# Picking the experts' inputs with the one-hot matrix stationary, and other edits at the ends of the stages

## The chip, the cores and the metric

The program runs on one core of a Trainium2 chip. The metric is the device time of one execution in microseconds (us). Each kernel is timed in several runs; one more execution is taken by the hardware profiler, and the rows below come from it. TensorE multiplies, with its weight loads beside it (PEld); VectorE (DVE), ScalarE (ACT) and GpSimd (POOL) work on the tiles; SyncE (SP) and GpSimd issue most of the transfers (DMA).

## The reference

One layer of an encoder on 256 tokens of 2048 channels, all in float32:

```
h = rms_norm(x) ; proj = h @ w_in
q, k, v, q_idx, k_idx, w_idx | r, d_w, kr, vr, d_a, d_g = split_cols(proj)
y_dsa  = sparse attention: 8 heads of 128; an indexer keeps the best min(256, L/4) = 64
         keys of each query, chunks of 64, RMS-norm and rotary on q and k
y_rwkv = RWKV-7: 16 heads of 64; token shift, decay and gates of low rank;
         state = state * w + (state @ -kk) b^T + v k^T ; y = state @ r
x = x + concat(y_dsa, y_rwkv) @ w_out
t = rms_norm(x)
grp = top-1 of 4 groups ; two of its 4 experts, weights p_grp * p_exp / sum
x = x + sum over 16 experts e of combine[:, e] * ((silu(t @ gate_e) * (t @ up_e)) @ down_e)
```

An expert is three matrices of 2048 x 512, 512 x 2048 for the last; the sixteen together are 201 MB and are read in every run.

## The kernel before

**Order of the work.** TensorE's instructions are in an order that the program writes out by hand, while it is built; the other engines' orders are planned around it. A small planner (`Order`, L45) keeps a clock that each product moves on by an assumed price. `drive` (L399) goes through the stream of weight tiles (a task is one such tile with its 6 or 12 products) and between two tasks lets every chain go on whose time or event has come: the RWKV block chains (`rwkv_early`, `rwkv_late`), the attention, the norms. A chain's `yield` is either a wait in us (the list `Y`) or the name of an event. A task can need events (`od.need`); then the planner steps its clock and writes out what the chains have, with no task between.

**RWKV.** Eight blocks of two heads. `rwkv_early(b)` makes the products `pa` (L605) and hands a triangular system to `solve` (L653): it goes out to DRAM by GpSimd's queue, comes back spread over the lanes, is solved in 62 operations of GpSimd, goes out again and comes back as `XT` (L669). `solve` sets the event `solved{b}` SOLVE_US = 54 us later on the planner's clock (L670). `rwkv_late(b)` waits for it; its first product, `pz` on `XT` (L688), is the first use. Only one late chain is under way at a time. `rwkv_early(b)` waits for `late{b-2}` in its middle (L558). A late chain ends in a tile `r{b}` of the output projection's input, split into two parts (L899 and L900).

**Output projection.** The 2048 input channels stand in sixteen slots, `YSLOTS`: r0 to r5, h0 to h3, r6, h4 to h7, r7 (r for RWKV's blocks, h for the attention's heads). The 2048 output columns are done in four groups `c0` to `c3` of sixteen tasks, six products of 512 columns each; a task needs its slot's event. AHEAD = 10: the stream takes ten tasks of c0, ten of c1, and then the last six of each (L197).

**Experts.** After the projection come the norm, the routing and, while VectorE routes, WARM products that compute nothing. Each expert gets 64 slots of tokens; experts go in eight pairs, and a one-hot matrix `sel` (tokens x 128 slots) picks a pair's tokens. `gather(p)` (L1323) makes the turned inputs in four quarters of 512 channels: 8 products of a tile of the residual stream `uu` (128 x 128, stationary) with `sel` (128 columns, moving), both in float32, then a scale by `gF` on VectorE into `xe` (L1338); and at the end the turned `sel` and the factors. `up(p)` (L1356) has four quarters `kg`, each with 8 products for `gate` and 8 for `up`, and calls the generators of `gather` in between: the first two quarters of a pair are picked ahead of the down projection of the pair before, the others inside `up`. `down` (L1390) turns the hidden tile and makes four groups `pd` of 512 columns; `scatter` (L1409) brings them back to the tokens with products on two exact parts (`yh`, `yl`, type float32r) and adds them to `x1`. Output leaves by SyncE's queue.

**Weights.** The experts' weights come as 192 tiles of 1 MB, 24 a pair, in a ring (`load_chunk`, L1079): EB = 20 lasting places and three that are used once. A tile's transfer waits for the product that read its place last. The first tiles are loaded in the background of the projections, GpSimd's queue issuing; once the experts run, SyncE's. The last four tiles go in quarters.

What the program writes between `up(p)` and the next pair:

```
up(p, pend)
if p < 7:
    next(turns[p + 1])
    next(turns[p + 1])
_, selT, sv = got.pop(p)
```

Of the kernel before, what the change touches and what calls it, by code (L numbers as in the profile page):

```python
# [31 lines left out]
AHEAD = 10  # L32
EB1, EB2, EB = 9, 4, 20
# [3 lines left out]
PACE, SOLVE_US, RSTD_US = 2.2, 54.0, 16.1  # L37
# [80 lines left out]
def block_kernel(ctx: ExitStack, tc: tile.TileContext, a: dict, dbg=None):  # L118
# [960 lines left out]
    def load_chunk(i, gate=False):  # L1079
# [3 lines left out]
        elif i in once:  # L1083
            t = wp.tile([P, 2048], F32, name="ewr", tag="rawA")
        elif k < 3:
            t = gp.tile([P, 2048], F32, name="ew0", tag=f"g{k}")
        elif k < EB1:
            t = ewp[1].tile([P, 2048], F32, name="ew", bufs=EB1 - 3)
        elif k < EB1 + EB2:
            t = ewp[2].tile([P, 2048], F32, name="ew2", bufs=EB2)  # L1090
        elif k < EB1 + EB2 + 4:
            t = big.tile([P, 2048], F32, name="ewh", tag=f"h{k - EB1 - EB2}")
        elif k < EB1 + EB2 + 6:
            t = wp.tile([P, 2048], F32, name="eww", tag=f"w2{k - EB1 - EB2 - 4}")
        else:
            t = ewp[3].tile([P, 2048], F32, name="ew3", bufs=EB - EB1 - EB2 - 6)
# [43 lines left out]
    def u_chain(cc, ps):  # L1140
        cs = slice(cc * 512, (cc + 1) * 512)
        uu, lg, us = mo_["uu"], mo_["lg"], mo_["us"]
        for j in range(2):
            o = uu[:, j, cs]
            DVE.tensor_tensor(out=o, in0=o, in1=ps[j], op=ALU.add)
            sq = us.tile([P, 512], F32, name="usq", bufs=1)
            ACT.activation(out=sq, in_=o, func=AF.Square, accum_out=mo_["ssq"][:, j, cc:cc + 1])
        yield Y[34] if cc == 0 else Y[35]
        uT = us.tile([P, 4, T], F32, name="uT", bufs=1)
        for j in range(2):  # L1150
# [3 lines left out]
            ACT.copy(out=uT[:, :, j * P:(j + 1) * P], in_=pt.rearrange("p (i t) -> p i t", i=4))  # L1154
            if j == 0 and cc < 3:
                yield Y[20]
        yield Y[21]
# [73 lines left out]
    mx, sums, mxe, sme = sm_("mx", 1), sm_("sums", 4), sm_("mxe", 4), sm_("sme", 4)  # L1231
    ge = l[:, :, 4:20].rearrange(g4, g=4)
# [3 lines left out]
    DVE.tensor_tensor(out=l[:, :, 0:4], in0=l[:, :, 0:4], in1=mx.broadcast_to([P, 2, 4]), op=ALU.subtract)  # L1236
    DVE.tensor_tensor(out=ge, in0=ge, in1=mxe.rearrange(bc, o=1).broadcast_to([P, 2, 4, 4]), op=ALU.subtract)
# [60 lines left out]
    ewp[3] = ctx.enter_context(tc.tile_pool(name="ew3", bufs=1, reuse_waits="tile"))  # L1298
# [10 lines left out]
    def experts():  # L1309
# [13 lines left out]
        def gather(p):  # L1323

            sel = md.tile([P, 2, P], F32, name="sel")
            for e in range(2):
                for j in range(2):
                    DVE.tensor_scalar(sel[:, j, e * 64:(e + 1) * 64], iota, pos[:, j, 2 * p + e:2 * p + e + 1], selm[:, j, 2 * p + e:2 * p + e + 1], ALU.is_equal, ALU.mult)  # L1328
            xe = []
            got[p] = [xe, None, None]  # L1330
            for kq in range(4):
# [5 lines left out]
                t = XE[0][:, (kq % 2) * 512:(kq % 2 + 1) * 512].rearrange("p (a t) -> p a t", t=P)  # L1337
                DVE.tensor_tensor(out=t, in0=ps.rearrange("p (a t) -> p a t", t=P),  # L1338
                                  in1=gF[:, 4 * kq:4 * kq + 4].rearrange("p (a o) -> p a o", o=1).broadcast_to([P, 4, P]), op=ALU.mult)
                xe.append(t)  # L1340
                yield
            ps = misc()
            for j in range(2):
                tr(ps[:, j * P:(j + 1) * P], sel[:, j, :])
            for j in range(2):
                mm(ps[:, T:T + 17], sel[:, j, :], val[:, j, :], start=(j == 0), stop=(j == 1))
            selT = md.tile([P, T], F32R, name="selT")
            sv = md.tile([P, 2], F32, name="sv", bufs=2)
            ACT.copy(out=selT, in_=ps[:, 0:T])  # L1349
            DVE.tensor_copy(sv[:, 0:1], ps[:, T:T + 1])  # L1350
            for e in range(2):
                DVE.tensor_copy(sv[64 * e:64 * e + 64, 1:2], ps[64 * e:64 * e + 64, T + 1 + 2 * p + e:T + 2 + 2 * p + e])
            got[p][1:] = selT, sv
            yield

        def up(p, pend):  # L1356
            pgt = pg_.tile([P, 512], F32, name="gate", bufs=1)
            put = pg_.tile([P, 512], F32, name="up", bufs=1)
            for kg in range(4):
                w = {}  # L1360
                xe = got[p][0]
                for m, o in ((0, pgt), (1, put)):
# [13 lines left out]
                if kg < 2:  # L1376
                    next(turns[p])
                if kg == 1:
                    next(turns[p])
            sv = got[p][2]  # L1380
            if not R:
                R.append(wp.tile([P, 2048], F32, name="R", tag="rawA"))
                XE[0] = R[0][:, 1024:2048]
                Y2.append(wp.tile([P, 1024], F32R, name="Y2", tag="rawB"))
# [5 lines left out]
        def down(sv):  # L1390
            hh, hT = R[0][:, 0:512], R[0][:, 512:1024]
            yh, yl = Y2[0][:, 0:512], Y2[0][:, 512:1024]
# [4 lines left out]
            for n in range(4):  # L1397
                pd = pg_.tile([P, 512], F32, name="pd", bufs=2)
                w = [nxt() for _ in range(2)]
                for kt in range(4):  # L1400
                    if kt == 2:
                        yield n
# [6 lines left out]
        def scatter(selT, n, first, final):  # L1409
            yh, yl = Y2[0][:, 0:512], Y2[0][:, 512:1024]  # L1410
            ns = slice(n * 512, (n + 1) * 512)
            for j in range(2):
                ps = pg_.tile([P, 512], F32, name="sc", bufs=2)
# [3 lines left out]
                if final:  # L1417
                    SP.dma_start(out=outv[:, j, ns], in_=x1[j][:, ns])
# [4 lines left out]
        next(turns[0])  # L1423
        pend = None
        for p in range(8):
            up(p, pend)
            if p < 7:
                next(turns[p + 1])
                next(turns[p + 1])
            _, selT, sv = got.pop(p)  # L1430
            prev = None
            for n in down(sv):
                if prev is not None:
# [5 lines left out]
        scatter(*pend, False, True)  # L1439
# [112 lines left out]
```

## Time and profile before

| | us |
|---|---|
| median of 3 runs | 1066.7 (1066.42 to 1069.66) |
| the profiled execution | 1065.43 |
| its span, first to last instruction | 1063.3 |
| TensorE busy | 1015.9 (96%) |
| VectorE busy | 536.6 (50%) |
| ScalarE busy | 386.4 (36%) |
| GpSimd busy | 287.2 (27%) |
| moved by DMA | 298.75 MB, mean 281 GB/s |

The span lies inside the execution's time. The projections and the mixers take it up to about 590 us, the experts run from 605 us to the end. A busy time says that an engine worked, not that something waited for it; for that the timelines, the waits and the chain of work are read. In a timeline row the bracket at the end is the idle time of the engine ahead of the instruction, with what ended it.

### The profile page before, as it was taken

The numbers are of one execution on the slowest core, as the hardware profiler recorded it, in microseconds if no ns is written. First come the engines' busy times: TensorE is split into PE (matmuls) and PEld (weight loads), VectorE is DVE, ScalarE is ACT, GpSimd is POOL, SyncE is SP. The second block draws the span as 40 slices with busy tenths as digits, with TensorE's granted clock in tenths as the row PEclk, the third lists the DMA queues.
The fourth block names the chain that finished last, engine by engine and source line by source line (L and its number), as shares of the span: only waits on it lengthen the run. The fifth ranks groups of instructions, "written<-read, shape, count | busy, mean of one in ns | idle before, by whom it ended". The sixth has DMA issues, their size and how long they took to land.

```text
span 1063.3 us, 17241 instructions
## 1 busy us (share of the span) xinstructions
PE 1015.9 (96%) x6466; PEld 685.3 (64%) x6466; DVE 536.6 (50%) x1195; ACT 386.4 (36%) x816; POOL 287.2 (27%) x705
## 2 busy tenths in 40 slices
PE   7899999999999999799899899999999999999997
PEld 6888988887888987687678644444444444444432
DVE  5796868697958786956444413122221223131313
ACT  6755655666557674656344201010000000010101
POOL 4106672658166825573043110000000000000000
PEclk9999999999999999999999999999999999999999
DMA  9556654454546554456389999999999999999995
GB/s 310 194 184 182 185 162 159 113 161 117 166 140 182 156 148 136 128 164 210 98 302 349 421 420 371 419 421 419 419 421 419 421 419 420 420 419 420 420 415 206
DMA packets 61754, 298.75 MB, mean 281 GB/s; under 512 B 8960, under 2 KB 12336, under 8 KB 37600
## 3 DMA queue, kind: packets, MB, share of 16 engines
q1 hardware_dynamic: 51264, 251.21, 63.7%
q0 software_dynamic: 10400, 46.36, 12.3%
q8 instruction: 53, 0.87, 0.3%
q14 instruction: 37, 0.30, 0.1%
HBM read 294.37 MB, written 3.15 MB: 280 GB/s over the span
## 4 chain that ended last, share of the span: by engine, by line
PE 73%; DVE 4%; ACT 2%; issue 1%; DMA 1%; ACTq 0%; DVEq 0%
PE pp L131 23%; PE pd L131 11%; PE gate L131 11%; PE up L131 10%; PE misc L131 6%; PE sc L131 3%; PE pz L131 2%; PE py L131 2%; DVE W L207 1%; DMA RB<-wo 1%; ACT W L206 1%; PE pc L131 1%; PE lps L131 1%; PE yps L131 1%; PE misc L141 1%
## 5 line engine op out<-in xcount | busy, mean ns | idle before, releaser
L131 PE MATMUL pp<-W,hT 128*128 128x512 f32 x768 | 189.7, 398 | 1.6 <-DVE W L207 1.6
L131 PE MATMUL pp<-hT,W 128*128 128x256 f32 x1296 | 171.6, 289 | 12.3 <-ACT W L206 8.6
L207 DVE TENSOR_TENSOR W<-RA,W 128x512 fp32r<-128x512 f32 x200 | 137.8, 695 | 83.6 <-ACT W L206 82.1
L131 PEld LDWEIGHTS pp<-hT,W 128*128 128x128 f32 x1296 | 161.7, 194 | 17.1 <-ACT W L206 8.8
L206 ACT CAST W<-RA 128x512 fp32r<-128x512 f32 x200 | 123.1, 620 | 119.9 <-PE pp L131 87.4
L131 PEld LDWEIGHTS pp<-W,hT 128*128 128x128 f32 x768 | 141.2, 189 | 32.1 <-DVE W L207 2.0
L131 PE MATMUL pp<-W,yT 128*128 128x512 f32 x384 | 95.5, 403 | 3.5 <-ACT yT L899 3.3
L666 POOL TENSOR_TENSOR xt<-xt,tt 128x24 f32<-128x24 f32 (+23 forms) x248 | 91.8, 370 | 19.3
L664 POOL TENSOR_TENSOR tt<-xt,at 128x24 f32<-128x24 f32 (+23 forms) x248 | 86.0, 347 | 40.0 <-DMA at<-din 21.3
L207 DVE TENSOR_TENSOR W<-RB,W 128x512 fp32r<-128x512 f32 x100 | 69.3, 696 | 43.7 <-ACT W L206 42.1
L131 PEld LDWEIGHTS pp<-W,yT 128*128 128x128 f32 x384 | 72.1, 192 | 20.7 <-ACT yT L899 3.5
L206 ACT CAST W<-RB 128x512 fp32r<-128x512 f32 x100 | 61.5, 619 | 64.6 <-PE pp L131 51.3
L131 PE MATMUL pd<-ew,R 128*64 128x512 f32 x352 | 81.1, 598 | 2.7 <-ACT R L1396 2.7
L131 PE MATMUL up<-ew,R 128*64 128x512 f32 x352 | 79.3, 592 | 0.0
L131 PEld LDWEIGHTS misc<-sel,uu 128*128 128x128 f32 x512 | 59.6, 192 | 15.2 <-issue 13.8
L1406 ACT ACTIVATE Y<-pd,sv 128x512 fp32r<-128x512 f32 x32 | 22.0, 687 | 126.9 <-PE pd L131 126.9
L1407 DVE SCALAR_TENSOR_TENSOR Y<-pd,sv,Y 128x512 fp32r<-128x512 f32 x32 | 24.0, 750 | 83.1 <-ACT Y L1406 83.1
L131 PE MATMUL misc<-sel,uu 128*128 128x128 f32 x512 | 63.0, 278 | 0.7 <-DVE sel L1328 0.7
L1416 DVE TENSOR_TENSOR x<-x,sc 128x512 f32<-128x512 f32 x56 | 36.0, 684 | 55.0 <-PE sc L131 55.0
L131 PE MATMUL gate<-ew,R 128*64 128x512 f32 x272 | 61.7, 595 | 0.0
L1338 DVE TENSOR_TENSOR R<-misc,gF 128x512 f32<-128x512 f32 x28 | 19.4, 692 | 79.5 <-PE misc L131 79.5
L1349 ACT CAST selT<-misc 128x256 fp32r<-128x256 f32 x8 | 3.0, 372 | 154.5 <-PE misc L131 154.5
(383 smaller groups left out, 1253.6 us busy)
## 6 DMA issues: line engine op xcount, KB each, us to landing
ew<-we SPq DMA_DIRECT2D x66, 1024.0 KB, 19.9
ew<-wdn SPq DMA_DIRECT2D x38, 1024.0 KB, 18.7
ew<-we POOLq DMA_DIRECT2D x25, 1024.0 KB, 10.6
ewh<-we SPq DMA_DIRECT2D x24, 1024.0 KB, 17.8
RA<-wd SPq DMA_DIRECT2D x43, 512.0 KB, 3.6
RA<-wr SPq DMA_DIRECT2D x35, 512.0 KB, 4.5
RB<-wd SPq DMA_DIRECT2D x21, 512.0 KB, 3.7
RA<-wo SPq DMA_DIRECT2D x21, 512.0 KB, 4.1
```

The source lines that it names most:

```text
L131: PE.matmul(out, lhsT=lhsT, rhs=rhs, start=start, stop=stop, skip_group_check=skip)
L141: PE.transpose(out=out, in_=in_, identity=ident)
L206: ACT.copy(out=hi, in_=raw)
L207: DVE.tensor_tensor(out=lo, in0=raw, in1=hi.bitcast(F32), op=ALU.subtract)
L664: POOL.tensor_tensor(out=tv, in0=xt[:, 0:n, s_:s_ + 1].broadcast_to([P, n, m]), in1=at[s_ >= 8][:, s_ % 8 if s_ < 8 else s_ - 8, s_ + 1:32 ...
L666: POOL.tensor_tensor(out=xt[:, 0:n, s_ + 1:32], in0=xt[:, 0:n, s_ + 1:32], in1=tv, op=ALU.subtract)
L1338: DVE.tensor_tensor(out=t, in0=ps.rearrange("p (a t) -> p a t", t=P), in1=gF[:, 4 * kq:4 * kq + 4].rearrange("p (a o) -> p a o", o=1).broa ...
L1349: ACT.copy(out=selT, in_=ps[:, 0:T])
L1406: ACT.activation(out=yh, in_=pd, func=AF.Copy, scale=sv[:, 1:2])
L1407: DVE.scalar_tensor_tensor(out=yl, in0=pd, scalar=sv[:, 1:2], in1=yh.bitcast(F32), op0=ALU.mult, op1=ALU.subtract)
L1416: DVE.tensor_tensor(out=x1[j][:, ns], in0=(uu[:, j, ns] if first else x1[j][:, ns]), in1=ps, op=ALU.add)
```

## The change

- `gather`: pairs 0 and 1 keep the old pick (`direct`; pair 1 for its first half). From then on a quarter of `uu` is first split into two exact parts of type float32r (`parts`: a copy on ScalarE, a difference on VectorE, for each half of the tokens); `pick` has `sel` stationary and moves the parts, four products of 512 columns, ScalarE copies the result, `turned` transposes it in four products, and VectorE scales as before. The generator's steps are called at other places of `up`.
- Pair 0's first quarter is scaled in two halves.
- The pool of split parts takes the place of one ring slot: EB from 20 to 19.
- SOLVE_US from 54 to 47, AHEAD from 10 to 14.
- In the last group of the output projection the sums of squares come after the turned tiles, and the second copy is on VectorE. The routing has two VectorE operations fewer.
- The last down group goes in two halves of 256 columns; the output's second half of the tokens leaves by ScalarE's queue.

```diff
-AHEAD = 10
-EB1, EB2, EB = 9, 4, 20
+AHEAD = 14
+EB1, EB2, EB = 9, 4, 19
-PACE, SOLVE_US, RSTD_US = 2.2, 54.0, 16.1
+PACE, SOLVE_US, RSTD_US = 2.2, 47.0, 16.1
...
+        if cc == 3:
+            for j in range(2):
+                squares(j)
...
-    DVE.tensor_reduce(mx[:, :, 0], l[:, :, 0:4], axis=AX.X, op=ALU.max)
-    DVE.tensor_reduce(mxe, ge, axis=AX.X, op=ALU.max)
...
+    DVE.tensor_reduce(mx5, l5, axis=AX.X, op=ALU.max)
...
+            def parts(kq):
+
+                two = []
+                for j in range(2):
+                    t, o = md.tile([P, 2, 512], F32R, name="two", bufs=2), uu[:, j, kq * 512:(kq + 1) * 512]
+                    ACT.copy(out=t[:, 0, :], in_=o)
+                    DVE.tensor_tensor(out=t[:, 1, :], in0=o, in1=t[:, 0, :].bitcast(F32), op=ALU.subtract)
+                    two.append(t)
+                return two
+
+            def pick(two):
+
+                ps = misc()
+                for j in range(2):
+                    for n in range(2):
+                        mm(ps, sel_r[:, j, :], two[j][:, n, :], start=(j == 0 and n == 0), stop=(j == 1 and n == 1))
+                E = wp.tile([P, 512], F32, name="E", tag="rawB")
+                ACT.copy(out=E, in_=ps)
+                return E
+
+            def turned(kq, E):
+                ps = misc()
+                for i in range(4):
+                    tr(ps[:, i * P:(i + 1) * P], E[:, i * P:(i + 1) * P])
+                xe.append(scaled(kq, ps, 0, 4))
...
+            else:
+                two = parts(0)
+                yield
+                E = pick(two)
+                two = parts(1)
+                yield
+                turned(0, E)
+                E = pick(two)
+                two = parts(2)
+                turned(1, E)
             yield
...
+                E = pick(two)
+                two = parts(3)
+                yield
+                turned(2, E)
+                yield
+                E = pick(two)
+                factors()
+                yield
+                turned(3, E)
+                yield
...
-                        if p == 0 and kg == 0:
-                            next(turns[0])
+                        if p == 0 and kg == 0 or p and kg == 1:
+                            next(turns[p])
+                        if kg == 2 and p:
+                            next(turns[p])
+                        if kg == 2 and p < 7:
+                            next(turns[p + 1])
+                        if kg == 3 and p < 7:
+                            next(turns[p + 1])
...
+                if final and n == 3:
+                    for hf in range(2):
+                        cs = slice(hf * 256, hf * 256 + 256)
...
-                    SP.dma_start(out=outv[:, j, ns], in_=x1[j][:, ns])
+                    (SP, ACT)[j].dma_start(out=outv[:, j, ns], in_=x1[j][:, ns])
```

## Rows read from the trace of the kernel before

**Rows 1.** The page's slices: what the transfers moved in each of 40 slices.
```profile
GB/s 310 194 184 182 185 162 159 113 161 117 166 140 182 156 148 136 128 164 210 98 302 349 421 420 371 419 421 419 419 421 419 421 419 420 420 419 420 420 415 206
```

**Rows 2.** Windows: stretch, length, busy time of the engines, granted clock, DMA share, GB/s.
```profile
440.00:460.00 20.00, 14.46 (x89) 11.54 (x87) 15.76 (x34) 7.13 (x17) 8.45 (x14) 0.83 0.42 116
520.00:540.00 20.00, 14.42 (x111) 10.78 (x110) 6.77 (x15) 5.65 (x15) 6.30 (x17) 0.83 0.41 136
...
650.00:655.00 5.00, 5.00 (x24) 1.87 (x22) 2.04 (x3) 0.69 (x1) 0.00 (x0) 1.00 0.71 259
...
960.00:1020.00 60.00, 59.33 (x312) 27.26 (x308) 14.04 (x26) 4.40 (x7) 0.00 (x0) 1.00 1.01 420
...
1047.00:1048.00 1.00, 1.00 (x6) 0.34 (x6) 1.00 (x2) 0.00 (x0) 0.00 (x0) 1.00 0.40 143
```

**Rows 3.** Timeline of TensorE, 446 to 545: start, duration, instruction [idle before it].
```profile
446.10 0.89 PE L131 MATMUL pa<-G 64*64 64x128 f32 x24 [0.96 <-DVE G L584]
...
503.98 5.74 PE L131 MATMUL pp<-W,yT 128*128 128x512 f32 x24
509.56 1.05 PE L131 MATMUL pz<-R,XT 128*128 128x128 f32 x8
510.45 2.78 PE L131 MATMUL yps<-PT,vt 128*128 128x256 f32 x16
512.99 1.64 PE L131 MATMUL pp<-W,yT 128*128 128x512 f32 x6
...
522.91 0.33 PE L131 MATMUL pS<-S,Ph 64*64 64x64 f32 x4 [0.40 <-ACT S L727]
...
532.07 11.96 PE L131 MATMUL pp<-W,yT 128*128 128x512 f32 x42 [3.27 <-ACT yT L899]
```

**Rows 4.** Timeline: block 0's solve on TensorE and GpSimd, block 7's on GpSimd.
```profile
74.54 1.10 PE L131 MATMUL pa<-G 64*64 64x128 f32 x32
...
122.98 2.21 POOL L669 DMA_DIRECT2D XT<-dout  x4 [3.80 <-DMA dout<-xt]
...
129.89 1.05 PE L131 MATMUL pz<-R,XT 128*128 128x128 f32 x8
...
490.17 2.18 POOL L669 DMA_DIRECT2D XT<-dout  x4 [3.84 <-DMA dout<-xt]
```

**Rows 5.** The tile `XT`, 50 to 160: from issue to landing.
```profile
DMA to landing us min/median/max: 2.5/3.3/3.9
```

**Rows 6.** Timeline of TensorE around the down projections of two successive pairs.
```profile
866.18 3.84 PE L131 MATMUL misc<-sel,uu 128*128 128x128 f32 x32
869.86 0.60 PE L141 MATMUL misc<-ident,R 128*128 128x128 f32 x4
871.13 5.37 PE L131 MATMUL pd<-ew,R 128*64 128x512 f32 x24 [0.68 <-ACT R L1396]
876.43 1.20 PE L131 MATMUL sc<-Y,selT 128*128 128x512 f32 x4
...
922.09 3.84 PE L131 MATMUL misc<-sel,uu 128*128 128x128 f32 x32
```

**Rows 7.** Timeline: SyncE's issues of weights, TensorE's first down groups of the last pair.
```profile
651.19 5.51 SPq L1106 DMA_DIRECT2D ewh<-we  x4
...
1009.05 7.79 SPq L1106 DMA_DIRECT2D ew<-wdn  x4
...
1036.19 5.37 PE L131 MATMUL pd<-ew,R 128*64 128x512 f32 x24 [0.68 <-ACT R L1396]
```

**Rows 8.** DMA issues, 1003 to 1018: tile, count, KB, median us to landing.
```profile
ew<-wdn SPq DMA_DIRECT2D x4, 1024.0 KB, 19.9
```

**Rows 9.** The chain of work that ended last: the first scale of the experts.
```profile
607.23 0.70 DVE XE L1338
```

**Rows 10.** Timeline of VectorE at the end.
```profile
1056.11 1.28 DVE L1416 TENSOR_TENSOR x<-x,sc 128x512 f32<-128x512 f32 x2 [0.59 <-PE sc L131]
```

**Rows 11.** The tensor `out`: from issue to landing.
```profile
DMA to landing us min/median/max: 2.3/3.3/6.0
```

More of the change, by code (lines that the diff above doesn't have):

```diff
@@ L1142, in u_chain, with squares @@
         uu, lg, us = mo_["uu"], mo_["lg"], mo_["us"]
+        def squares(j):
+            sq = us.tile([P, 512], F32, name="usq", bufs=1) if cc < 3 else ppbank()
+            ACT.activation(out=sq, in_=uu[:, j, cs], func=AF.Square, accum_out=mo_["ssq"][:, j, cc:cc + 1])
         for j in range(2):
@@ L1342, in gather @@
[L1342 to L1352, printed above, removed]
@@ new lines, in factors @@
+            def factors():
+                ps = misc()
+                for j in range(2):
+                    tr(ps[:, j * P:(j + 1) * P], sel[:, j, :])
+                for j in range(2):
+                    mm(ps[:, T:T + 17], sel[:, j, :], val[:, j, :], start=(j == 0), stop=(j == 1))
+                selT = md.tile([P, T], F32R, name="selT")
+                sv = md.tile([P, 2], F32, name="sv", bufs=2)
+                ACT.copy(out=selT, in_=ps[:, 0:T])
+                DVE.tensor_copy(sv[:, 0:1], ps[:, T:T + 1])
+                for e in range(2):
+                    DVE.tensor_copy(sv[64 * e:64 * e + 64, 1:2], ps[64 * e:64 * e + 64, T + 1 + 2 * p + e:T + 2 + 2 * p + e])
+                got[p][1:] = selT, sv
@@ L1379, in up @@
                     next(turns[p])
+                    if p == 0:
+                        next(turns[p])
             sv = got[p][2]
@@ L1399, in down @@
                 w = [nxt() for _ in range(2)]
+                if final and n == 3:
+                    for hf in range(2):
+                        cs = slice(hf * 256, hf * 256 + 256)
+                        for kt in range(4):
+                            if kt == 2 and hf == 0:
+                                yield n, 0, 512
+                            for e in range(2):
+                                mm(pd[64 * e:64 * e + 64, cs], hT[:, kt * P + 64 * e:kt * P + 64 * e + 64], w[e][:, kt * 512 + hf * 256:kt * 512 + hf * 256 + 256], start=(kt == 0), stop=(kt == 3))
+                        ACT.activation(out=yh[:, cs], in_=pd[:, cs], func=AF.Copy, scale=sv[:, 1:2])
+                        DVE.scalar_tensor_tensor(out=yl[:, cs], in0=pd[:, cs], scalar=sv[:, 1:2], in1=yh[:, cs].bitcast(F32), op0=ALU.mult, op1=ALU.subtract)
+                    yield n, 0, 256
+                    break
                 for kt in range(4):
                     if kt == 2:
-                        yield n
+                        yield n, 0, 512
                     for e in range(2):
@@ L1422, in experts @@
         turns = [gather(p) for p in range(8)]
-        next(turns[0])
+        for _ in range(3):
+            next(turns[0])
         pend = None
@@ L1428, in experts @@
                 next(turns[p + 1])
-                next(turns[p + 1])
             _, selT, sv = got.pop(p)
             prev = None
-            for n in down(sv):
-                if prev is not None:
+            for n, c0, c1 in down(sv, p == 7):
+                if c1 < 512:
+                    scatter(selT, n, False, True, c0, c1)
+                elif prev is not None:
                     if not base and p == 0 and n == 1:
@@ L1438, in experts @@
             pend = prev
-        scatter(*pend, False, True)
+        scatter(*pend, False, True, 256, 512)
     experts()
```

70 lines of the change are left out of this document (45 added, 25 removed).

## The prediction

> **What bounds the kernel now.** I read the page's slices first: from the 23rd slice on, the transfers move 420 GB/s and never more [rows 1], and the windows of the expert stage show the same 420 GB/s with TensorE busy 59.33 of 60 us at full clock [rows 2]. So two things run side by side there, and it matters which is ahead. One pair of experts takes 24 tiles of weights of 1 MB; SyncE issues one each 2.49 us (four in 7.79, of which the last takes 0.33) [rows 7], so a pair's weights need 59.8 us, while TensorE needs 55.9 us: the pick ahead of the down projection recurs at 866.18 and 922.09 [rows 6]. TensorE therefore eats up its stock of loaded tiles by 3.9 us a pair. At the end little is left: the two tiles of the last pair's second down group are issued last at 1016.5 and land 19.9 us later [rows 7, 8], at 1036.4; TensorE starts on them about 1039.7 (16 of the 24 instructions that begin at 1036.19) [rows 7]. The stock is 3.3 us deep there, and the last bytes land at 1047 [rows 2]. **Whatever TensorE saves in the expert stage, 3.3 us of it can show, unless the stream itself ends sooner.**
>
> Ahead of the experts TensorE works almost without a break, but for two holes: 440 to 460 and 520 to 540, in each of which it is busy only 14.4 of 20 us and the granted clock is 0.83 [rows 2], that is (1 - 0.83) x 20 / 0.5 = 6.8 us at 1.2 GHz. The second hole is the last block's late chain: tiles of the output projection that need no late result run out, TensorE idles, and goes on at 532.07 when the last head's result is split (ACT yT) [rows 3]. Idle: 20 - 14.42 = 5.6 us. After it 42 instructions take 11.96 us, where 24 took 5.74 [rows 3], so 42 should take 10.0: 1.9 us lost to the lower level. Together 7.5 us.
>
> The profiled run took 1065.4 us (span 1063.3); the median of the timed runs is 1066.7, so 1.3 us go onto the result of the sum.
>
> **The change, part by part.**
>
> *Planner constants* (SOLVE_US 54 to 47). The planner puts a block's late chain 54 us after its triangular solve is sent off; for block 0 this is real time: products `pa` end at 75.6, the first product on the solve's result starts at 129.9, 54.3 later [rows 4]. With 47 it is written 7 us earlier, at 122.6 plus up to a tile, say 123.5. But the solve's result is sent at 122.98 in four transfers of 0.55 us issue, which land up to 3.9 us after issue [rows 4, 5], so about 128.4. TensorE is in order: it stands 4.9 us (4.0 to 5.5), and the projection's tiles queued behind this product stand with it. A hole of 5.6 us cost 1.9 more by the clock; I add the same: +6.8. Block 7 has its `pa` done at 447.0, its result sent at 490.2 to 492.4, so landed by 496, 49 us after, and used at 509.56, 63 us after [rows 3 to 5]; 7 us less costs such a block nothing. What it gives: block b+2 starts only when late b is done, so every second block gains another 7 us: late 1, 3, 5, 7 by 7, 14, 21, 28 on the planner's clock, less the 6.8 lost at block 0, so the last one some 20 us. Then the hole at 520 to 540 has filler: -7.5.
>
> *AHEAD 10 to 14.* The output projection now asks for heads h4 to h6 of the attention as its 12th to 14th tile and not after 20. Those heads' products stand at 510.45, and their tile follows directly at 512.99 [rows 3]: they come just in time for the 22nd tile now. Asked for ten tiles (ten times 1.43 = 14 us) sooner, less the 7 to 14 us of late products that now stand before, they are late by up to 7 us or not at all; the planner then writes the rest of the chain without filler. Bounds 0 and 12.2 (the late chain without filler, 522.5 to 532.07, is 9.6 long [rows 3]; with the clock's 1.9, and 0.7 for one more round of the heads, 12.2); I take 4.5, nearer to zero, because those heads run through TensorE and need no round over GpSimd.
>
> *The hole at 440 to 460* comes from ScalarE and VectorE, crowded by late 5, early 7 and the attention at once. Late 5 now ends some 14 us sooner (21 less 6.8). Bounds: all of it stays (0), or all goes (5.5 + 1.9 = -7.4); I take -4.8. **Front: -7.5 + 6.8 + 4.5 - 4.8 = -1.0** (between -8 and +9).
>
> *Start of the experts.* The last Squares go behind the turned tiles and one copy goes to VectorE: between nothing and one ScalarE operation of 512 columns (the 0.68 of the copy's wait [rows 6]), I take 0.45; the first scale in halves: half of 0.70 [rows 9]. TensorE starts 0.8 us sooner. The two VectorE operations saved in routing lie beside the warm-up products and give nothing.
>
> *One ring slot less (EB 20 to 19).* At the first down projection the ring is full: SyncE's first issue stands at 651.19, when the first `pd` group frees its slots [rows 7]; DMA falls to 0.71 in 650 to 655 [rows 2]. With one slot less each tile behind that point lands one tile later against TensorE's clock: 2.5 us, of which the 0.8 us earlier start gives back its part: **+1.7** on the end of the stream. It also means that earlier prefetching ahead of the experts buys nothing: the stream is set anew by this slot.
>
> *The pick.* Before: 16 instructions in 1.9 us for four columns of tiles (3.84 for 32) [rows 6], four times a pair. After, from pair 2 on: four products of 512 columns as the scatter has them (1.20, or 1.14 to the next instruction) and four transposes (0.60; 0.45 when another product follows) [rows 6]: 1.6. Two such picks and their turns ahead of the down projection, with ScalarE's copy between (before the down projection such a copy leaves TensorE idle 0.68 [rows 6]): 0.45 + 1.14 + 0.68 + 0.45 instead of 3.84, 1.1 less; three picks and two turns in the middle of `up` instead of two picks: 0.5 more. A pair gains 0.6, six pairs 3.4 (bounds: 0 if VectorE orders its work badly, 2.5 a pair without any wait). ScalarE and VectorE take eight more operations each a pair of about 0.7; they have room, busy 4.4 and 14 of 60 us [rows 2]. With the 0.8 of the start TensorE is 4.2 us sooner at the last pair, but the stock is 3.3 deep and the stream 1.7 later: only 3.3 - 1.7 = **1.6 counts**; the other 2.6 us become waits for `ew`.
>
> The Trainium skill (DMA: Bandwidth & Descriptors, Where 436 GB/s comes from) puts the ceiling of a core's transfers at 435 GB/s. By it the stream could end (1 - 420/435) x 387 (660 to 1047) = 13 us sooner and the whole pick would pay; the trace's 420 in every full window speaks against it.
>
> *The end.* The last group in halves: its scaling on ScalarE and VectorE and its adds (1.28 for two, so 0.64 for 512 columns of one [rows 10]; I take the scalings as long) are half as long behind the last product, but the first half's adds stand in between: 1.1 in all; the products in halves take up to 0.6 longer, I say 0.15. Output of 128 KB and not 256, landing now 2.3 to 6.0 after issue [rows 11], and issued by two engines: 0.8. **-1.8** (-0.3 to -2.8). The Trainium skill (same page, Rules for kernel authors) has it that a second issuing engine saves issue time alone; then it is 1.3.
>
> **Sum:** -1.0 - 1.6 - 1.8 = -4.4: 1065.4 becomes 1061.0 in a profile, 1062.3 in timed runs.
>
> **Rivals.**
> 1. *The holes all go*: no wait for h4, the hole at 440 closes: front -7.5 + 6.8 - 7.4 = -8.1, so 1066.7 - 8.1 - 3.4 = 1055. For it: filler is plentiful once the last chain is early. Against: the tiles ask for h4 ten places sooner.
> 2. *Slower: the output projection waits for the attention.* The tile c0[11] is written before h4 is there, the rest of attention and of the last late chain follow without filler, the upper bound of 12.2: front -7.5 + 6.8 + 12.2 - 4.8 = +6.7, 1066.7 + 6.7 - 3.4 = 1070. It decides from a wait of about 8.9 (level) and costs over 0.3% from 12.1; if the hole at 440 stays, from 7.3.
> 3. *Not what it says: the saving isn't taken.* The pair gains nothing (waits between copy and turn) and the front comes out at +1 to +3: 1065 to 1067.
>
> **How the numbers follow.** Forecast 0.45, centred on 1062.3 (1059 to 1066); rival 1: 0.20; rival 2: 0.22; rival 3: 0.13. A measurement of this kernel tells 0.3% (3.2 us) from no change: faster is below 1063.5, slower above 1069.9. Faster: three quarters of the forecast (0.33) and rival 1: 0.53; slower 0.22; same 0.25. Range 1053.5 to 1070: it takes in rival 1 and reaches to rival 2.
>
> **What would show it.** TensorE idle about 5 us at 123 to 128 before `pz<-R,XT`, with a granted clock below 1 in that window; the hole at 520 to 540 gone and one ahead of a `pp<-W,yT` behind h4's split; 420 GB/s through the expert stage and, in the last pair only, TensorE waiting for `ew` (some 2.6 us in all); a pair at some 55.3 us. Wrong if TensorE waits for no weights at the end, if the stream exceeds 420, or if the front differs from before by over 8 us either way.

## The result, and the profile after

The changed kernel takes 1077.7 us (median of 6 runs, 1069.6 to 1079.3) where the kernel before takes 1068.3 beside it: a ratio of 1.0070 (95% interval 1.0051 to 1.0089), taken over the runs; the two medians alone would give 1.0088, since two of the six runs lie well below the other four. The forecast was 1062.3, range 1053.5 to 1070. It is slower, and its runs lie wider apart (9.8 us against 3.2). The trace is of the lowest run, 1069.6 (span 1067.7, mean granted clock 0.993); the other five have 0.984 to 0.988. Times and ratios below are of runs in the chip's faster state, which leaves out one of the ten runs of e4_ahead10, of 1074.1 us.

The windows of [rows 2], in the kernel after (stretch, length, busy time of PE, PEld, DVE, ACT, POOL, granted clock, DMA share, GB/s):

```profile
440.00:460.00 20.00, 19.98 (x160) 16.44 (x159) 15.52 (x29) 13.86 (x35) 13.21 (x31) 1.00 0.46 127
520.00:540.00 20.00, 19.09 (x80) 14.55 (x80) 7.84 (x13) 7.76 (x14) 3.58 (x8) 1.00 0.98 334
650.00:655.00 5.00, 5.00 (x24) 1.82 (x20) 0.94 (x2) 0.69 (x1) 0.00 (x0) 1.00 0.32 107
960.00:1020.00 60.00, 58.59 (x269) 22.65 (x269) 19.45 (x34) 10.79 (x19) 0.00 (x0) 1.00 1.01 419
```

Both holes of [rows 2] are gone, at full clock. The missing ring slot shows at 650 (DMA share 0.32, where it was 0.71), and the stream runs at the same 419 to 420 GB/s after it. What came in place of the holes is in TensorE's waits from 120 to 470 (waited for, us in total, times, longest):

```profile
PE tps L141 <- DVE MM L609: 3.0, 2, 1.7
PE py L131 <- DVE S L738: 2.8, 1, 2.8
PE pz L131 <- DMA XT<-dout: 2.4, 1, 2.4
PE ptp L141 <- DVE L L921: 2.0, 1, 2.0
PE ips L131 <- DVE MM L609: 1.6, 1, 1.6
```

Block 0's wait is there (`pz`, 2.4), and four rows of waits for VectorE, 9.4 us, that stand at places where no wait was forecast. All of TensorE's waits for VectorE in these 350 us come to 10.4 us; in the kernel before they come to 9.2, of which 5.5 are the hole at 440. That hole closed, but waits of more than its length stand elsewhere. In the projection's stretch, TensorE's timeline (start, duration, instruction, idle before it):

```profile
498.40 1.64 PE L131 MATMUL pp<-W,yT 128*128 128x512 f32 x6
...
511.09 18.34 PE L131 MATMUL pp<-W,yT 128*128 128x512 f32 x79
529.66 2.79 PE L131 MATMUL pp<-W,yT 128*128 128x512 f32 x11 [0.23 <-DVE W L207]
532.90 0.50 PE L131 MATMUL pp<-W,yT 128*128 128x512 f32 x1 [0.45 <-ACT W L206]
...
545.54 0.64 PE L131 MATMUL pl<-uT,wrt 128*32 128x256 f32 x8 [2.56 <-issue]
```

From 500 to 511 the last late chain and the attention run with no product of the projection between them; after it TensorE waits for split weights `W`. The wait ahead of `pl` is ScalarE's: its copy of `uT` stands behind a split whose weight tile landed late:

```profile
543.34 1.14 ACT L206 CAST W<-RA 128x512 fp32r<-128x512 f32 x2 [1.39 <-DMA RA<-wo]
544.38 1.06 ACT L1160 COPY uT<-utp 128x512 f32<-128x512 f32 x2
```

A pair of experts, from the middle of `up` to the next down projection (answers to [rows 6]):

```profile
903.30 0.66 PE L141 MATMUL misc<-ident,E 128*128 128x128 f32 x4
903.88 3.65 PE L131 MATMUL up<-ew,R 128*64 128x512 f32 x16
907.47 1.20 PE L131 MATMUL misc<-two,sel 128*128 128x512 f32 x4
...
920.36 1.19 PE L131 MATMUL misc<-two,sel 128*128 128x512 f32 x4
921.48 3.65 PE L131 MATMUL up<-eww,R 128*64 128x512 f32 x16
925.07 0.66 PE L141 MATMUL misc<-ident,E 128*128 128x128 f32 x4
925.48 1.17 PE L131 MATMUL misc<-two,sel 128*128 128x512 f32 x4
927.38 0.66 PE L141 MATMUL misc<-ident,E 128*128 128x128 f32 x4 [0.73 <-ACT E L1375]
927.87 0.60 PE L141 MATMUL misc<-ident,R 128*128 128x128 f32 x4
929.15 1.08 PE L131 MATMUL pd<-ew,R 128*64 128x512 f32 x4 [0.68 <-ACT R L1487]
```

The down projection recurs at 873.06 and 929.15, every 56.09 us; it was 55.91 (871.13 to 927.04). And the end, on TensorE and VectorE:

```profile
1056.78 0.43 PE L131 MATMUL pd<-ewh,R 128*64 128x256 f32 x1 [1.37 <-DVE Y L1500]
...
1060.40 0.62 PE L131 MATMUL sc<-Y,selT 128*128 128x256 f32 x3 [0.28 <-DVE Y L1500]
```

```profile
1060.82 0.75 DVE L1519 TENSOR_TENSOR x<-x,sc 128x256 f32<-128x256 f32 x2 [0.48 <-PE sc L131]
```

The second half of the last group waits 1.37 us for the first half's scaling. From the last pair's first down product (1038.31; before 1036.19 [rows 7]) to the end of the span it is 29.4 us, where it was 27.1.

### The profile page after: what moved, and what is told of

Read it like the earlier page. It is cut to its first block, busy times and chain, and to the rows that moved or that the text cites. A ratio compares the mean times of both kernels' runs of the same rounds, so it can differ in the third digit from the quotient of the medians.

```text
span 1067.7 us, 17050 instructions
## 1 busy us (share of the span) xinstructions
PE 1013.0 (95%) x6278; PEld 665.5 (62%) x6278; DVE 569.9 (53%) x1250; ACT 426.1 (40%) x894; POOL 289.1 (27%) x704
## 3 DMA queue, kind: packets, MB, share of 16 engines
q10 hardware_dynamic: 720, 1.05, 0.3%
## 4 chain that ended last, share of the span: by engine, by line
PE 62%; DMA 12%; DVE 5%; ACT 2%; issue 1%; ACTq 0%; POOL 0%; DVEq 0%; SPq 0%
PE pp L131 22%; PE pd L131 8%; PE up L131 8%; PE gate L131 8%; DMA ew<-we 4%; PE misc L131 3%; PE sc L131 3%; DMA RB<-wo 3%; DMA ewh<-wdn 2%; DMA ew<-wdn 2%; DMA eww<-we 2%; PE py L131 2%; DVE W L207 2%; PE pz L131 2%; PE misc L141 2%
## 5 line engine op out<-in xcount | busy, mean ns | idle before, releaser
L664 POOL TENSOR_TENSOR tt<-xt,at 128x24 f32<-128x24 f32 (+23 forms) x248 | 88.4, 356 | 42.8 <-DMA at<-din 24.2
L131 PE MATMUL pd<-ew,R 128*64 128x512 f32 x344 | 84.3, 598 | 3.4 <-ACT R L1487 3.4
L1363 ACT CAST two<-uu 128x512 fp32r<-128x512 f32 x52 | 32.1, 620 | 118.2 <-PE misc L131 118.2
L131 PE MATMUL up<-ew,R 128*64 128x512 f32 x288 | 72.7, 596 | 0.0
L131 PE MATMUL gate<-ew,R 128*64 128x512 f32 x304 | 72.6, 595 | 0.0
L1519 DVE TENSOR_TENSOR x<-x,sc 128x512 f32<-128x512 f32 (+1 forms) x58 | 36.2, 665 | 56.4 <-PE sc L131 56.4
L1364 DVE TENSOR_TENSOR two<-uu,two 128x512 fp32r<-128x512 f32 x52 | 35.8, 690 | 34.9 <-ACT two L1363 34.9
L131 PEld LDWEIGHTS pd<-ew,R 128*64 128x64 f32 x344 | 24.2, 136 | 46.4 <-issue 41.6
L131 PEld LDWEIGHTS gate<-ew,R 128*64 128x64 f32 x304 | 22.0, 137 | 41.9 <-issue 41.1
## 6 DMA issues: line engine op xcount, KB each, us to landing
ew<-we SPq DMA_DIRECT2D x63, 1024.0 KB, 19.9
ew<-wdn SPq DMA_DIRECT2D x41, 1024.0 KB, 19.9
```

The costliest lines, as they stand in the source:

```text
L131: PE.matmul(out, lhsT=lhsT, rhs=rhs, start=start, stop=stop, skip_group_check=skip)
L664: POOL.tensor_tensor(out=tv, in0=xt[:, 0:n, s_:s_ + 1].broadcast_to([P, n, m]), in1=at[s_ >= 8][:, s_ % 8 if s_ < 8 else s_ - 8, s_ + 1:32 ...
L1363: ACT.copy(out=t[:, 0, :], in_=o)
L1364: DVE.tensor_tensor(out=t[:, 1, :], in0=o, in1=t[:, 0, :].bitcast(F32), op=ALU.subtract)
L1519: DVE.tensor_tensor(out=x1[j][:, ns], in0=(uu[:, j, ns] if first else x1[j][:, ns]), in1=ps, op=ALU.add)
```

## The experiments

Every run is timed against the kernel before on the same chip; ratios with their 95% interval. The runs were made in five groups, and the median of the kernel before lies between 1066.7 and 1068.5 us in them; the row of before has the time beside the first four runs, and the columns at the end from its first trace. "New" experts are the changed kernel's pick, ring and end; "old" are those of before, with the moved squares, the shorter routing and the halved first scale kept.

| run | SOLVE_US | AHEAD | experts | us | ratio | idle | half | first gate |
|---|---|---|---|---|---|---|---|---|
| before | 54 | 10 | | 1067.7 | 1 | 33.2 | 13.7 | 608.0 |
| e2_front_old | 54 | 10 | new | 1070.0 | 1.0018 (1.0000 to 1.0036) | 33.2 | 13.7 | 609.0 |
| e3_solve54 | 54 | 14 | new | 1078.5 | 1.0098 (1.0059 to 1.0137) | 41.8 | 20.5 | 619.3 |
| e1_same | 47 | 14 | new | 1074.9 | 1.0071 (1.0032 to 1.0110) | 38.1 | 17.1 | 613.9 |
| e4_ahead10 | 47 | 10 | new | 1064.8 | 0.9981 (0.9952 to 1.0010) | 31.0 | 10.2 | 602.2 |
| e7_pick_old | 47 | 10 | old, new end | 1060.6 | 0.9940 (0.9902 to 0.9978) | 30.5 | 13.7 | 603.3 |
| e11_front | 47 | 10 | old | 1065.3 | 0.9970 (0.9949 to 0.9991) | 35.5 | 23.9 | 612.3 |
| g5_front_49 | 49 | 10 | old | 1061.1 | 0.9949 (0.9930 to 0.9967) | 32.1 | 17.1 | 608.4 |
| e12_front_50 | 50 | 10 | old | 1049.7 | 0.9826 (0.9807 to 0.9845) | 21.7 | 6.8 | 591.3 |
| g3_solve50 | 50 | 14 | new | 1055.9 | 0.9886 (0.9868 to 0.9904) | 25.7 | 3.4 | 595.3 |
| g4_front_51 | 51 | 10 | old | 1052.7 | 0.9877 (0.9848 to 0.9906) | 22.9 | 6.8 | 593.5 |
| g6_front_52 | 52 | 10 | old | 1064.6 | 0.9984 (0.9972 to 0.9995) | 33.4 | 13.7 | 605.9 |
| g1_block0_50 | 47, block 0: 50 | 10 | old | 1061.8 | 0.9933 (0.9909 to 0.9957) | 31.4 | 13.7 | 606.6 |
| g2_block0_47 | 50, block 0: 47 | 10 | old | 1059.6 | 0.9923 (0.9907 to 0.9940) | 28.0 | 10.2 | 602.6 |

The last three columns are of each run's trace: TensorE's idle time before the first `gate` product, the time in that stretch at the half level of the clock (0.50), and when that product starts. The start less the idle time less half of the time at the half level is 564.7 to 569.6 us in all 20 traces, where the start itself lies between 591.3 and 619.3: the work in the front is the same, and the differences are waits of TensorE and the lower clock, within 5 us.

**The two constants of the front.** `e1_same` is the changed kernel again; the others set SOLVE_US to 54, AHEAD to 10, or both.

> The changed kernel once more, unaltered. Its six times lay between 1069.6 and 1079.3 us and the one trace shows the lowest of them (mean granted clock 0.993; the others 0.984 to 0.988). By the clock theory, a run of about 1077 us has two or three more stretches of some 6.8 us at the half level than the trace of the 1069.6 us run, each worth 3.4 us, and no longer waits elsewhere: 1077 - 1069.6 = 7.5 = 2.2 such stretches. By the rival (the slow runs wait for something, weights or GpSimd's solve), the TensorE idle time before the experts, 28.1 us, is several us longer in such a run. Expected median 1076 to 1078.

> SOLVE_US 54 and AHEAD 10 as in the kernel before; everything from the output projection's end on stays changed. If the front constants bring the loss in the timed runs: the first gate product stands at about 607 to 608, as before, the experts and the end keep what they lost in the trace (0.9 in the pairs, 2.3 in the last pair's end): 1071 to 1072 us. If the experts bring it (waits there that lower the clock): 1076 to 1078 us, as the changed kernel.

> SOLVE_US back to 54, AHEAD stays 14. If SOLVE_US = 47 (block 0's products stand 2.4 us for the solve, others in the holes that follow) is what costs in the front: as with both undone, 1071 to 1072, no wait for XT at block 0. If AHEAD = 14 is: 1076 to 1078, with the hole at 520 to 540 back and deeper, since the attention's heads are asked for ten tasks sooner while the late chain is late.

> AHEAD back to 10, SOLVE_US stays 47. If SOLVE_US = 47 is what costs in the front: 1076 to 1078. If AHEAD = 14 is: 1070 to 1072, and the front is shorter than both: the late chains 20 us sooner and no task that waits for h4.

Measured: 1074.9, 1070.0, 1078.5, 1064.8. AHEAD = 14 costs 8.5 us with 54 and 10.1 with 47; SOLVE_US = 47 gains 3.6 with AHEAD 14 and 5.2 with 10; what is left of the change, 1070.0 against 1067.7, costs 2.3. (One way from before to the changed kernel, -5.2 + 10.1 + 2.3, gives its 7.2 by construction; that the two constants nearly add up shows in the two values of each.) By the intervals, AHEAD's cost is clear both times, the 3.6 is not clear of noise, and the 5.2 and the 2.3 barely are. The theory that the experts bring the whole loss falls. On the run of 1074.9 both theories held a part: 6.8 us more at the half level than in the first trace (3.4 us of time) and 3.3 more idle, 2.4 of it a wait for block 7's solve.

With 54 and AHEAD 14 the standstill of the second rival is there. In the trace of e3_solve54 TensorE waits 6.0 us in all for the last chains' results ahead of the projection's products (3.3 in e2_front_old), and 5.8 us more ahead of the turned tiles, which it doesn't in e2_front_old. That wait is for the residual stream: VectorE adds to `uu`, which is loaded late, behind an issue on GpSimd's queue that had waited 47.0 us for a late chain's `yT`:

```profile
552.17 1.28 DVE L1148 TENSOR_TENSOR uu<-uu,pp 128x512 f32<-128x512 f32 x2 [3.68 <-DMA uu<-x]
552.96 1.94 PE L141 MATMUL utp<-ident,uu 128*128 128x128 f32 x8 [5.84 <-DVE uu L1148]
```

The two together are 8.5 us more than in e2_front_old, about all that AHEAD costs with 54. With 47 there is no such standstill, and the cost has to be found elsewhere.

**Late weights, or a chain without filler?** AHEAD 14 and SOLVE_US 47, with the background loading slowed:

```diff
-PACE, SOLVE_US, RSTD_US = 2.2, 47.0, 16.1
+PACE, SOLVE_US, RSTD_US = 6.6, 47.0, 16.1
```

> The changed kernel (AHEAD 14, SOLVE_US 47), with the background loading of expert weights during the output projection slowed: one tile in 6.6 tasks, not in 2.2. From the first product on yT to the first gate product the changed kernel takes 129.4 and 132.0 us in its two traces; with AHEAD 10 it takes 122 to 128. If AHEAD 14 costs because the projection's own weights then come late beside the experts' (4.3 us of longer gaps between its products, 2.6 to 3.0 us for ScalarE, which stands on such a tile ahead of a copy): these waits are gone and the stretch is 122 to 125 us, 1067 to 1070 in timed runs. If it costs because the last late chain runs without filler: the waits may go, but the stretch stays above 128 and the time at 1074 or more.

Measured: 1080.1 (1.0100, 1.0075 to 1.0125). What ScalarE waits for during the projection, in the changed kernel (511 to 597), in e4_ahead10 (519 to 589) and in e9_pace (513 to 597):

```profile
ACT W L206 <- DMA RA<-wo: 16.3, 8, 3.8
ACT W L206 <- DMA RB<-wo: 14.8, 6, 3.3
```

```profile
ACT W L206 <- DMA RA<-wo: 14.9, 7, 3.5
...
ACT W L206 <- DMA RB<-wo: 4.6, 3, 2.2
```

```profile
ACT W L206 <- DMA RA<-wo: 9.6, 4, 3.3
ACT W L206 <- DMA RB<-wo: 4.7, 2, 2.5
```

31.1 us against 19.5 and 14.3: the projection's weights do come late beside the experts', and slowing those mends it. From the first product on yT to the last the projection takes 117.1 and 119.7 us in the two traces with AHEAD 14, 109.5 to 113.9 in seven with 10 (110.7 in e4_ahead10), and 114.6 here: 2.5 to 5 us of the loss were the late weights. Some 1 to 5 us stay; that these are the chain without filler and its wait ahead of `pl` is argued from the timeline and not shown by a run of its own. What the slower loading gained was lost again later, as no theory had it: GpSimd still has tiles to issue when the routing needs it, and its copy of `ps` (and TensorE behind it) waits in line:

```profile
606.23 0.53 POOL L1102 DMA_DIRECT2D ewh<-wdn  x1 [3.52 <-DMA ewh<-wdn]
608.71 0.53 POOL L1102 DMA_DIRECT2D eww<-wdn  x1 [1.95 <-DMA ew<-we]
609.23 0.20 POOL L1250 COPY ps<-lp 128x8 f32<-128x8 f32 x1
...
612.15 0.58 PE L131 MATMUL pps<-selm,utri 128*128 128x16 f32 x2 [5.50 <-DVE p L1285]
```

**The end and the pick**, each on e4_ahead10. `e5_tail_old` undoes the halves and the second output queue. `e6_tail_banks` gives the second half its own PSUM tile (in it the third group's parts are overwritten before they are scattered; the work is the same):

```diff
+                        if hf:
+                            yield n, 0, 512
+                            pd = pg_.tile([P, 512], F32, name="pd", bufs=2)
                         for kt in range(4):
-                            if kt == 2 and hf == 0:
-                                yield n, 0, 512
```

> Base: the changed kernel with AHEAD 10 (e4_ahead10); the last down group undivided and all output by SyncE's queue, as in the kernel before. In e4_ahead10 the span ends 28.9 us after the last pair's first down product; in the kernel before 27.1. If the halves are what costs (a wait of 1.36 between them, and their adds and scalings in turn): 27.1 +- 0.3. If the end is later for another reason (weights later, a slower output): 28.5 or more.

> Base e4_ahead10; the second half of the last down group in its own PSUM tile, and the scatter of the third group between the halves. If the second half waits because it shares its tile with the first, which ScalarE and VectorE still read: the 1.36 us wait ahead of the second half is gone and the span ends 27.0 to 27.5 after the last pair's first down product (28.9 in e4_ahead10). If it waits for something else (the order of VectorE): the wait stays.

Measured (one run each, 1064.6 and 1064.1): 27.5 and 28.1 us from the last pair's first down product to the span's end (28.9 in e4_ahead10). Over all traces it is 27.1 to 27.8 with the old end (ten), 28.3 to 30.2 with the halves (eight), 28.1 and 27.3 with the halves in two tiles. To VectorE's last add, without the output, it is 21.2 with the old end (as before), 22.9 with the halves, 22.1 with the halves in two tiles. With two tiles no product of the second half waits. But the run also moved the third group's scatter between the halves, and the second half begins at 1051.55, after VectorE has read the first (1050.10 to 1050.58): which of the two took the wait away isn't separated. What speaks for the shared tile is the changed kernel's own row, where a product that reads nothing of the first half waits 1.37 us for that half's scaling. The Trainium skill (PSUM — Partial Sum Buffer, PSUM bank collisions raise a hardware error) says that two engines must not be in one bank at once; the halves share one, with their tile, and that row agrees. Even so the halves don't pay: scaling and adds of the first stand ahead of those of the second on VectorE, and in e6_tail_banks TensorE waits 0.60 us ahead of the moved scatter.

`e7_pick_old` takes the old pick and EB = 20; `e8_pick_late` adds e6's end (with the same overwriting) and puts the second quarter's pick behind the turn of the hidden tile:

```diff
             ACT.copy(out=hT, in_=ps)
+            if p < 7:
+                next(turns[p + 1])
...
             if p < 7:
                 next(turns[p + 1])
-                next(turns[p + 1])
```

> Base e4_ahead10; the old pick in all pairs, and EB 20 again; the rest stays changed. By the count of the cuts (six insertions between gate and up products in place of three, each 0.16 us, eat the 0.28 that picks and turns save): a pair takes 55.9 us, not 56.1, TensorE is 1.1 sooner at the last pair, and the stock of weights there is over 4 us, where it was 1.9: 1064 us in timed runs if e4_ahead10 has 1065.4. By the rival (the pair is longer because ScalarE and VectorE, or the weights, come late in it): a pair takes under 55.7, or stays at 56.1 with the old pick too.

> e7_pick_old with the end of e6_tail_banks, and the second quarter's old pick between the turn of the hidden tile and the down projection, where TensorE waits 0.68 us a pair for ScalarE's copy. If that wait can be filled: a pair takes 55.1 to 55.3, TensorE is 4 to 5 us sooner at the last pair than in e7_pick_old, and of that what the stock of weights allows shows (4 us): 1058 to 1060 us. If a new wait takes its place (the PSUM bank that VectorE has not yet read, or ScalarE's queue): 55.8 to 55.9 and 1062 to 1064.

Measured: a pair takes 55.90 us in e7_pick_old and 56.09 in every trace with the new pick. Counted from start to start over one pair: picks and turns 7.44 before, 7.16 after (four picks 5.08, of which one waits 0.73; four turns 2.08), so 0.28 saved; the eight groups of `gate` and `up` 27.84 before, 28.3 after, so 0.46 lost. A group with its like on both sides takes 3.43, with something else ahead of it 3.48, behind it 3.53, on both sides 3.58; three cuts became six. Of the 4.2 us between e7_pick_old and e4_ahead10 only 1.4 lie behind the first gate product (456.5 and 457.9 to the end); the rest is the front, whose time varies from run to run with 47. In e8_pick_late (1060.0; 0.9943, 0.9918 to 0.9967) a pair takes 55.77: the wait of 0.68 is gone, and most of it came back ahead of the last pick, for a PSUM tile that VectorE still reads:

```profile
919.15 0.60 PE L141 MATMUL misc<-ident,R 128*128 128x128 f32 x4
920.10 2.05 PE L131 MATMUL misc<-sel,uu 128*128 128x128 f32 x16 [0.35 <-DVE R L1343]
```

**The due time of the solve.** `e10_front_pace`, `e11_front` and `e12_front_50` go back to the old experts and the old end; the first has the slower loading, the last SOLVE_US = 50.

> SOLVE_US 47 and AHEAD 10, the old pick and EB 20, the old end and SyncE's queue alone, so that from the change only SOLVE_US, the moved squares, the routing and the halved first scale stay; and the slower background loading of e9_pace. If late tiles of the projection cost something with AHEAD 10 too (a 1.3 to 2.9 us wait ahead of pl in five traces): 2 us less than e11_front. If the ring then is not full in time: TensorE waits for weights in the first two pairs and it is slower.

> As e10_front_pace, with the loading as before (one tile in 2.2 tasks). By the sum of the parts: pairs of 55.9, the span's end 27.1 to 27.5 us after the last pair's first down product, 1 us less than e7_pick_old, so 1059 to 1061 us, 0.993 of before. If the end is no shorter than in e7_pick_old: 1060.5.

> e11_front with SOLVE_US 50. If the stall at block 0 (2 to 3 us before pz, with half clock after it in some runs) is what SOLVE_US 47 pays: no stall, and late 7 begins about 4 x 3 - 3 = 9 us later; with the holes at 440 and 520 still filled it is 2 to 4 us faster than e11_front. If the filler for the last late chain is what counts: part of the hole at 520 to 540 comes back and it is 1 to 5 us slower.

Measured: 1076.3 (1.0073, 1.0047 to 1.0100), 1065.3 and 1049.7. The first lost 8.0 us ahead of `pps`, as e9_pace. The second was not the 1059 to 1061 of the sum; its trace, of one of its slower runs (1069.6), has 5.6 us of wait at block 0. The third beats all: runs of 1048.5 to 1050.7, where e11_front's lie between 1058.3 and 1071.1. TensorE's waits from 120 to 470 in e11_front and in e12_front_50:

```profile
PE pz L131 <- DMA XT<-dout: 5.6, 1, 5.6
PE tps L141 <- DVE MM L609: 3.0, 2, 1.7
PE py L131 <- DVE S L738: 2.8, 1, 2.8
```

```profile
PE tps L141 <- DVE MM L609: 1.0, 1, 1.0
PE pv L131 <- DVE y__5136 L480: 0.5, 1, 0.5
```

The waits for VectorE are the larger part of the difference, and block 0's wait does not make them. In all ten traces with 47 TensorE waits 10.2 to 10.4 us in this stretch for VectorE, at the same products, while the wait at block 0 lies anywhere from 0.1 us (e4_ahead10) to 5.6. With 54 the waits for VectorE are 8.9 to 9.2, with 49 7.1 and with 52 9.3; with 50 (two traces) they are 2.5 and with 51 2.2. Of 50's gain over 47 some 8 us are these waits. In the same stretch the clock is at the half level for 3.4 to 20.5 us with 47, and never with 50 or 51.

What parts the two, block 0's wait or the later blocks' order (the edit of g1_block0_50, on 47; g2_block0_47 has 50 and - 3.0):

```diff
-        od.event(f"solved{b}", SOLVE_US)
+        od.event(f"solved{b}", SOLVE_US + 3.0 * (b == 0))
```

> e11_front (SOLVE_US 47) with block 0's event alone set at 50 us. If the stall at block 0 is the cause: no wait for XT there, the later waits of 1.3 to 2.8 us are gone or small, and the time is 1049 to 1053. If the order of the later blocks is the cause: the stall at block 0 goes, the later waits stay, and 1060 to 1064 is left.

> e12_front_50 (SOLVE_US 50) with block 0's event alone at 47 us. If the stall at block 0 is the cause: 2 to 5 us of wait for XT, the later waits of 1.3 to 2.8 back, 1060 to 1066. If the order of the later blocks is: the stall and its clock alone, 2 to 5 us more than e12_front_50, 1052 to 1055.

> The changed kernel with SOLVE_US 50 and nothing else altered (AHEAD 14, the new pick, EB 19, the end in halves). The experts and the end cost 3.2 us against e12_front_50 by the traces. If AHEAD 14 costs the 8.5 to 9.5 us that it cost with 47 and 54: 1061 to 1063. If it costs nothing once the late chains are on time: 1052 to 1054. If SOLVE_US 47 was no part of the loss: 1074 or more.

> e12_front_50 with SOLVE_US 51. If what counts is that block 0 is not waited for and the last chain is early: as e12_front_50, 1048 to 1053. If 50 is a lucky order: anything up to the 1067 of 54.

> e12_front_50 with SOLVE_US 49. pz at block 0 is due at some 125.4 us and XT lands at 124.9 to 126 (125.8 in the changed kernel's trace): if TensorE's wait for the solve is what turns the time, little or no wait, 1050 to 1055. If 50 is a lucky order: 1058 to 1066, as at 47.

> e12_front_50 with SOLVE_US 52. No wait for any solve; each late chain 2 us later, so the last one 8 us later than at 50 and part of the hole ahead of the output projection's last tasks is back: 1053 to 1058, between 51 (1052.7) and the 1067 of 54. If 50 and 51 are lucky orders: 1060 or more.

Measured, in the order of the expectations: 1061.8, 1059.6, 1055.9, 1052.7, 1061.1 and 1064.6. Neither alone explains it: block 0 alone at 50 gives 3.5 of the 15.6 us, the others alone 5.8, together all (each within some 2 us). With block 0 on time, the wait moved to block 3 (and 2.4 us at block 4):

```profile
273.62 2.05 PE L131 MATMUL pz<-R,XT 128*128 128x128 f32 x8 [4.06 <-DMA XT<-dout]
```

From a block's first `pa` product to the last landing of its XT, the round takes 45.5 to 55.3 us over 20 traces, 124 of 160 times between 48 and 52, and 50.3, 48.6, 49.5, 50.5, 48.7, 52.0, 49.7 and 48.8 in e12_front_50, where `pz` stands 51.8 to 55.2 after `pa`. A due time of 47 puts `pz` 48.5 us after `pa` at the earliest (e4_ahead10), under many a round, so TensorE waited for a solve in every trace with 47 (0.1 to 5.6 us, and 6.4 with block 0 at 50); 50 and 51 lie above nearly all (no wait, but 0.8 in g3_solve50). At 49 the round of block 0 was 53.8 in the trace, and 3.4 us of wait came, and 7.1 us of waits for VectorE. At 52 I was wrong: no wait for a solve, but 1064.6. The last hole is back (3.3 us ahead of the projection at 529.75), and waits for VectorE of 3.7 and 2.2 us stand at 445 and 396. Both 49 and 52 came out where the expectations had put the rival that 50 is a lucky order, and that rival stands: the waits for the solve explain some of the loss below 50, but why VectorE is crowded at 47, 49, 52 and 54 and not at 50 and 51 is open. The changed kernel with 50 in place of 47 takes 1055.9, which shows what SOLVE_US is worth there: 19 us. Against e12_front_50 it has 6.2 us more, 3.8 of them in the experts (459.1 and 455.3 us from the first gate to the end), so AHEAD 14 costs some 2.4 with 50 by the medians (4.0 by the two traces' first gate), and not 8.5 to 10.1.

## Why the prediction was wrong

- **AHEAD: the term that failed most.** Taken as 4.5, measured 8.5 to 10.1; the second rival, at 12.2, was nearer. The step that failed is the choice "nearer to zero, because those heads run through TensorE". With 54 TensorE stood still for the last chains and for the residual stream, loaded behind them; with 47 the chain without filler came as that rival has it, without a standstill, and the products moved behind it ran into the stretch where the experts' loading fills the queues. Neither the late residual stream nor the late weights stood in the forecast.
- **SOLVE_US.** Forecast -5.5 (holes -7.5 and -4.8, block 0 +6.8); measured -5.2 and -3.6. The sum was near partly by luck, for two of its terms failed in opposite ways. Block 0's wait was priced at 4.9 and 1.9 for the clock, and was 2.4 with no lower clock in the first trace. The hole at 440 closed, but its 4.8 were not gained: TensorE is busy 5.5 us more from 440 to 460 and 7.7 less from 120 to 440 (307.0 us, before 314.7), and its waits for VectorE from 120 to 470 are 10.4 us, before 9.2. The hole at 520 went as forecast, with block 7 22 us sooner (487.6, 509.6 in [rows 3]). And "7 us less costs such a block nothing" is wrong: the 63 us at block 7 in [rows 3, 4] were queueing behind the chains before it, and once these are early, each block stands 0 to 8 us from its solve.
- **Start of the experts.** Forecast -0.8. From the projection's end to the first gate it takes 12.35, before 13.53, so -1.2 in this trace. But of the 19 traces with these edits eleven take 13.7, with 3.4 us at the half level of the clock in that stretch, so the gain is there only in runs where the clock stays up.
- **One ring slot less (EB).** Forecast one tile later, 2.5; the last byte lands at 1051.1, before at 1047.1, of which TensorE's later start is 1.2, so some 2.8. The stock at the last pair's second down group is 1.6 us (needed at 1041.80, issued at 1020.32 and 19.9 to landing), before 3.3. No wait of TensorE behind 1000 us is for a tile of weights, where 2.6 were forecast, as it was not faster; this was one of the forecast's own signs of being wrong. The ceiling of 435 GB/s that the Trainium skill states (DMA: Bandwidth & Descriptors, Where 436 GB/s comes from) was reached in no full window of the expert stage; 420 holds.
- **The pick.** Forecast -0.6 a pair, measured +0.18. Ahead of the down projection it saves 0.87 (4.08 from the first turn or pick to the down product, before 4.95; forecast 1.1); in the middle of `up` it costs 1.05 (forecast 0.5). The term left out is the cut: each costs the group of `gate` or `up` beside it some 0.15, the forecast priced none, and there are six, not three.
- **The end.** Forecast -1.8, measured +2.3. The products in halves cost 0.4 more (4.0 from start to start without the wait, before 3.6; forecast 0.15); the wait between them (1.37) and the two files on VectorE were not priced, and the output gained nothing: the last add to the span's end takes 6.1 us, before 5.9.
- Against the forecast in all: SOLVE_US +0.3, AHEAD +5.6, experts and end +5.7 (2.3 against -3.4).

The version that beats both is e12_front_50: the kernel before with SOLVE_US = 50, the moved squares, the shorter routing and the halved first scale, 0.9826 of before (0.9807 to 0.9845). From the first gate to the end it takes 455.3 us as before does; its gain is in the front.

## What to carry to other kernels

A due time written into a hand-made order must not lie under the real round that it stands for, and the round is measured in every block and several traces, with its spread: under it each run pays for the latency of that run. It also reorders every engine's work, so values around the round are tried and the waits for all engines counted: here 50 and 51 were good, and 49 and 52 took 8 to 15 us more. A cheaper operation put into a stream of products must be charged for each cut that it makes there. Work that is moved behind a chain is worth what the stretch costs in which it lands, its transfers included.

## What the runs showed of the hardware

- A wait of the same length cost different time: 2.9 us ahead of block 0's `pz` left the granted clock at 1.00 in e6_tail_banks, and went with 3.4 us at the half level in g2_block0_47 and 6.8 in e7_pick_old.
- How far the runs of one kernel lie apart went with SOLVE_US: nine and twelve runs with 47 span 13.6 and 12.8 us (e4_ahead10, e11_front), ten with 49 8.9; ten each with 52 and 54 4.3 and 4.6 (g6_front_52, e2_front_old), four with 50 2.3. Four with 51 span 7.0, by one run.
- The last output transfer takes 3.9 us from issue to landing at 128 KB (changed kernel, on ScalarE's queue) and 3.8 at 256 KB (before, on SyncE's): half the size saved nothing there. The three of 128 KB just ahead of it take 1.9 to 2.0, and those of 256 KB of the group before 2.3 and 2.6; what the last one waits for is open.
